# Adding a weight unit from DRAM onto its negated high part: a two-layer encoder on one core

## The chip, the core and the metric

The kernel runs on one core of one Trainium2 chip, as a single program. The metric is the device time of one execution in microseconds (us); lower is better. Five engines work side by side in it: PE multiplies matrices, DVE (vector), ACT (scalar) and POOL (GpSimd) work on tiles, and SP issues transfers from DRAM. Each engine takes its instructions in a fixed order and waits at an instruction until what it needs is there.

## What is computed

The reference is a two-layer encoder over 512 tokens of 1024 features, all in float32. Layer 0 mixes by trailing means and a causal convolution of width 31, layer 1 by chunked attention with 16 heads. Each layer ends in a gated feed-forward part with 2816 hidden features and a sigmoid gate on an input embedding.

```python
for i in range(DEPTH):
    j = i // 2
    if i % 2 == 0:
        mix = pool_conv_mixer(x, mix_w_in[j], pool_w[j], pool_scale[j], conv_dw_w[j],
                              conv_dw_b[j], conv_ln_g[j], conv_ln_b[j], mix_w_out[j])
    else:
        mix = chunked_rel_attention(x, attn_w_qkv[j], attn_rel_bias[j], attn_w_o[j])
    x = layer_norm(DEEPNORM_ALPHA * x + mix, ln_mix_g[i], ln_mix_b[i])
    ffn = conv_ffn(x, ffn_w_up[i], ffn_dw_w[i], ffn_dw_b[i], ffn_w_down[i])
    gate = jax.nn.sigmoid(x @ ple_w_gate[i] + ple_b_gate[i])
    ple = gate * (p[i] @ ple_w_proj[i])
    x = layer_norm(DEEPNORM_ALPHA * x + ffn + ple, ln_ffn_g[i], ln_ffn_b[i])
```

## The kernel before

**Products in three parts.** A float32 value is kept as a high part and a low part, both in the shorter format float32r, whose sum is the value. A product of two such values takes three matmuls (`mm3`, L84 to L86): high by high, low by high, high by low.

**Weights in units.** The weights, 205 units of mostly 128 x 1024 float32 (512 KB), come in the order of their use (the list `order`). The class `Weights` does this for each unit: SP loads it into one of three tiles `wraw` (L138), ACT copies it to `whi`, which rounds it to the high part (L80), and DVE subtracts `whi` from `wraw` and writes the low part `wlo` (L81). The two lines are in the helper `split_into`, which also splits activations, so L80 and L81 stand for those too; the tile names tell them apart. Up to seven units (`NB`) stand split or whole on chip. When the last product on a unit is issued, `free` calls `pump`, which writes the split of the next unit at that place. Units 8 to 11 (`WHOLE`) are loaded without a split.

**The stages.** In layer 0, products for the mixer run while the convolution's 31 taps are worked off in the background: by DVE (L518), and by a product on ACT (L511) with a sum on POOL (L512, 52 sums). DVE adds the two partial results at the end of a channel tile (L523). Then PE takes means over channels by products with ones (L660), DVE subtracts them (L663), and POOL takes the reciprocal root `rs4` (L677). In the feed-forward part every unit serves 24 products.

**The gate pipelines.** Between a mixer or feed-forward part and the stage behind it, `pipeline` works by token tiles of 128: residual sum, LayerNorm (DVE L335 and L336, with a small power on POOL, L330), transposes on PE (L347), and the first products of the next stage. In this stretch the subtract of four units is given to POOL (`W.eng = pool`), so that DVE is free for the LayerNorm.

**Attention.** Layer 1 loops over 16 heads. In one round PE computes scores of head i and transposes the probabilities of head i-1 (L817, tile `s`); ACT copies these to `ph` (L80), copies keys `kk` and queries `qh`, and takes the exponentials (L799); DVE takes a reciprocal `rc` (L801), by which POOL multiplies the four blocks of `s` (L805); PE's transposes of the next round need these. In between PE works through the projection of keys and queries, one unit per round. The order of PE, ACT, DVE and POOL in this part is fixed as written, by `pin`. Elsewhere a scheduler decides the order within each engine when the program is built.

Of the kernel before, what the change touches and what calls it, by code (L numbers as in the profile page):

```python
# [9 lines left out]
F32 = mybir.dt.float32  # L10
# [18 lines left out]
# k-tiles of the hidden layer that are on chip at a time  # L29
CHUNKS = (6, 8, 8)  # L30
# units of weights on chip: split, and as they come from DRAM
NB = 7
NRAW = 3
# the convolution's taps between two output tiles: by the vector engine, and by the scalar and pool engines
TICK = (6, 4)
# units that the splits are written behind while the convolution needs the vector engine
LAG = 2
# products on zeros before the first loads are there
WARM = 2
# units of weights that are used whole, in float32 products, for the vector engine's sake  # L40
WHOLE = (8, 9, 10, 11)
# an order of issue without a wait
# [5 lines left out]
# columns of the per-partition parameters  # L48
# [12 lines left out]
def trunk(ctx, tc, x, xt, pt, cols, w_in, w_pool, w_mo, w_qk, w_v, w_o, relb, rows, w_up, w_dn, w_pp, w_pg, out):  # L61
# [16 lines left out]
    # A float32 value is the exact sum of two float32r parts of 12 bits each.  # L78
# [11 lines left out]
    def pin(engines):  # L90
        """Keeps the order in which the engines' instructions since the last call are written here."""
        ins = nc.cur_bb.bb.instructions
        for eng in engines:
            prev = None
            for i in ins[mark[0] :]:
                if i.engine == eng.engine:
                    if prev is not None:
                        tc.add_manual_dep(i, prev.name, NOSYNC, reason="written order")
                    prev = i
        mark[0] = len(ins)  # L100

# [19 lines left out]
    class Weights:  # L121
        """Units of weights; each is loaded and split NB units ahead of its use."""
# [6 lines left out]
        def piece(self, n, cuts):  # L129
            """Loads unit n, or its part between the last two of the cuts."""  # L130
# [13 lines left out]
        def split(self, cuts=None):  # L144
            """Splits the next unit; with cuts a generator over its pieces."""
# [10 lines left out]
            for c1 in cuts or (n,):  # L156
                split_into(hi[:, c0:c1], lo[:, c0:c1], raw[:, c0:c1], self.eng)
# [31 lines left out]
    def fm_gen(o, a):  # L189
        """One output tile of 128 features with features on partitions; yields halfway."""  # L190
# [17 lines left out]
    def tm_mm(o, t, unit, kk, a, k0, first, last):  # L208
        """o[token, feature] += over k-tile kk of a unit, tokens on partitions."""
# [8 lines left out]
    def tm_units(o, a, ks, nk):  # L218
        """All token tiles, unit by unit, for k-tiles ks of nk; yields after each k-tile."""
# [10 lines left out]
    def tm_first(o, a, nk):  # L230
        """As tm_units for the first unit, a half of the tokens at a time."""
# [13 lines left out]
    class ByToken:  # L245
        """One token tile at a time, over the units of all k-tiles."""
# [19 lines left out]
    def pipeline(acc, pre, tr, mm, ev):  # L266
        """From the last products of a stage over its LayerNorm to the first products of the next, by token tiles."""
# [46 lines left out]
    class Norm:  # L314
        """LayerNorm of r over the features, in place."""
# [43 lines left out]
    class Gate:  # L359
        """r <- alpha r + sigmoid(x @ w_gate + b) * (p @ w_proj), half of the features."""  # L360
# [27 lines left out]
    def mix_to_gate(norm, by, gates):  # L388
        """The mixer's second half of features, LayerNorm and the gate's first half."""
# [13 lines left out]
    def feed_forward(i, nxt):  # L403
        """r <- LN(r + ffn(x)); then the products of nxt, or out."""
# [61 lines left out]
    with tc.tile_pool(name="mix", bufs=1, reuse_waits="tile") as mp:  # L466
        xr = [mp.tile([P, D], F32, tag="pp", name="xr", bufs=4) for _ in range(4)]
        # in the order of their first use
# [14 lines left out]
        # the scalar engine's table and the tensor engine's clock get ready while the first loads run  # L483
# [13 lines left out]
        # vector work that fills the gaps between the splits of the weights  # L497
        bg, convs, hs = deque(), deque(), []

        def tap(on_pool):  # L500
            """One more tap of the first channel tile that has one left: on the vector engine in PSUM, or
            with a product of the scalar engine and a sum of the pool engine."""
# [32 lines left out]
        def conv(c, pv, pg):  # L535
            """Gated linear unit of a channel tile; queues its convolution."""
# [10 lines left out]
        def window(g, pa):  # L547
            """Trailing mean of a channel group minus the group; queued."""
# [29 lines left out]
        # the first two tiles follow x as it comes in  # L578
# [44 lines left out]
        # the layer's input embedding, projected while the convolution runs  # L623
# [31 lines left out]
        # LayerNorm over the convolution's channels, which lie on partitions  # L655
# [13 lines left out]
        # the deviation's reciprocal with tokens on partitions, then again along them  # L669
# [29 lines left out]
    # per pair of heads: A's high part, A's low, B's low, B's high  # L699
# [16 lines left out]
    with tc.tile_pool(name="attn", bufs=1, reuse_waits="tile") as mp:  # L716
# [5 lines left out]
        # per head of a pair: the queries' high part twice; their low part where the keys' high part is, and zeros  # L722
# [5 lines left out]
        # probabilities by keys, the last key block after zeros  # L728
# [12 lines left out]
        def project():  # L741
            """Keys and queries of all pairs; yields after each half of a tile and after its split."""
            for p in range(NP):
# [3 lines left out]
                # a head's high part, and the low part on the other half of the partitions  # L747
# [59 lines left out]
        # keys on partitions, queries from the key's block on  # L807
# [41 lines left out]
        def fill():  # L849
            """Half a tile of projections, or a k-tile of the output projection once these are done."""  # L850
# [44 lines left out]
def _fm(w, np):  # L895
    """[1024, 128 G] -> units of eight k-tiles by 128 columns."""
# [73 lines left out]
```

## Time and profile before

| | before |
|---|---|
| median of 3 runs (lowest to highest), us | 1257.71 (1257.33 to 1257.73) |
| profiled execution: span from first to last instruction, us | 1259.6 |
| PE busy | 1222.5 us, 97% |
| DVE busy | 726.3 us, 58% |
| ACT busy | 490.7 us, 39% |
| POOL busy | 180.3 us, 14% |
| read from DRAM | 122.09 MB |
| share of the transfer engines, load queue | 29.7% |

The profiled execution is one execution apart from the three timed ones, and all durations come from it; the profile gives its span and no further time for it. A busy share is an average over stages with different limits, so PE's 97% leaves some 37 us in which PE is idle, and slower stretches in which the clock granted to it is below 1.00. Of that clock the profile gives the mean in a stretch, as a share of full speed.

### The profile page before, as it was taken

Reading aid. Unit: us, or ns where it says so; the run is one execution under the profiler, and the core shown is the slowest. Engines: PE = TensorE matmul, PEld = TensorE weight load, DVE = VectorE, ACT = ScalarE, POOL = GpSimd, SP = SyncE. Lnnn points to the kernel's source line nnn. Section 1 sums busy time; section 2 is a strip of 40 time slices with the busy share of each in tenths; the row PEclk is TensorE's granted clock in tenths of the full one; section 3 lists DMA queues with packets and bytes.
Section 4 is the critical chain, followed back from the end, with each engine's and each line's share of the span. In section 5 each row is a group of like instructions: output and inputs, shape, how many; then the busy total and the mean of one; then the engine's idle time right before and its main releaser. Section 6 shows DMA issues by size and latency. Waiting matters only on the chain.

```text
span 1259.6 us, 14166 instructions
## 1 busy us (share of the span) xinstructions
PE 1222.5 (97%) x5434; PEld 993.8 (79%) x5434; DVE 726.3 (58%) x1054; ACT 490.7 (39%) x742; POOL 180.3 (14%) x176
## 2 busy tenths in 40 slices
PE   8978999999999999999989999989999999999997
PEld 6735778888888888888878888868888888888886
DVE  6998595544444344449367777595544344434427
ACT  5654433432333123323257777322432233223320
POOL 2994040000000000004012323040000000000001
PEclk9998899999999999999999999999999999999999
DMA  8421232432233222332332232222422332223301
GB/s 308 171 70 50 67 108 77 151 100 88 97 100 101 97 89 99 101 108 97 127 103 76 76 91 78 67 89 96 130 89 99 100 100 92 93 101 100 98 19 67
DMA packets 36643, 125.11 MB, mean 99 GB/s; under 512 B 4064, under 2 KB 4448, under 8 KB 36576
## 3 DMA queue, kind: packets, MB, share of 16 engines
q1 hardware_dynamic: 36576, 124.20, 29.7%
q8 instruction: 43, 0.70, 0.2%
q14 instruction: 24, 0.20, 0.0%
HBM read 122.09 MB, written 2.10 MB: 99 GB/s over the span
## 4 chain that ended last, share of the span: by engine, by line
PE 85%; POOL 5%; DVE 4%; ACT 2%; issue 2%; DMA 1%; SPq 0%; DVEq 0%; POOLq 0%; ACTq 0%
PE psa L84 22%; PE psa L85 22%; PE psa L86 22%; PE psb L86 5%; PE psb L84 5%; PE psb L85 5%; POOL h L512 4%; PE psb L817 2%; DVE r L336 1%; PE psb L786 1%; PE psb L835 1%; PE psb L834 1%; DVE r L335 1%; PE psb L785 1%; POOL s L805 1%
## 5 line engine op out<-in xcount | busy, mean ns | idle before, releaser
L81 DVE TENSOR_TENSOR wlo<-wraw,whi 128x1024 fp32r<-128x1024 f32 (+3 forms) x191 | 239.1, 1252 | 323.5 <-ACT whi L80 317.1
L80 ACT CAST whi<-wraw 128x1024 fp32r<-128x1024 f32 (+2 forms) x203 | 211.6, 1043 | 464.9 <-PE psa L85 235.5
L84 PE MATMUL psa<-a0h,whi 128*128 128x512 f32 x896 | 350.2, 392 | 1.6 <-ACT a0h L80 1.6
L86 PE MATMUL psa<-a0h,wlo 128*128 128x512 f32 x896 | 349.2, 390 | 0.8 <-DVE wlo L81 0.8
L85 PE MATMUL psa<-a0l,whi 128*128 128x512 f32 x896 | 349.2, 390 | 0.0
L84 PEld LDWEIGHTS psa<-a0h,whi 128*128 128x128 f32 x896 | 168.6, 188 | 37.2 <-ACT a0h L80 2.5
L86 PEld LDWEIGHTS psa<-a0h,wlo 128*128 128x128 f32 x896 | 168.4, 188 | 36.6 <-DVE wlo L81 1.2
L85 PEld LDWEIGHTS psa<-a0l,whi 128*128 128x128 f32 x896 | 168.6, 188 | 34.5 <-DVE a0l L81 0.4
L330 POOL TENSOR_TENSOR rs<-ve,nhalf 128x1 f32<-128x1 f32 x16 | 15.1, 941 | 501.7 <-DVE ve L328 501.7
L512 POOL TENSOR_TENSOR h<-h,pr 128x512 f32<-128x512 f32 x52 | 82.7, 1598 | 24.4 <-ACT pr L511 21.3
L422 DVE TENSOR_TENSOR hr<-t,psa 128x512 f32<-128x512 f32 x44 | 30.3, 689 | 86.1 <-PE psa L86 83.1
L84 PE MATMUL psa<-whi,a1h 128*128 128x512 f32 x176 | 71.8, 408 | 6.3 <-ACT a1h L80 5.6
L85 PE MATMUL psa<-wlo,a1h 128*128 128x512 f32 x176 | 70.1, 398 | 0.0
L805 POOL TENSOR_TENSOR s<-s,rc 128x512 f32<-128x512 f32 (+1 forms) x64 | 47.8, 779 | 154.2 <-DVE rc L801 117.0
L86 PE MATMUL psa<-whi,a1l 128*128 128x512 f32 x160 | 63.3, 399 | 2.2 <-DVE a1l L81 2.2
L84 PE MATMUL psb<-whi,a1h 128*128 128x512 f32 x160 | 63.8, 399 | 1.5 <-ACT a1h L651 1.5
L84 PE MATMUL psa<-whi,a0h 128*128 128x512 f32 x160 | 63.7, 398 | 0.0
L85 PE MATMUL psb<-wlo,a1h 128*128 128x512 f32 x160 | 63.2, 395 | 0.0
L85 PE MATMUL psa<-wlo,a0h 128*128 128x512 f32 x160 | 62.9, 393 | 0.0
L86 PE MATMUL psa<-whi,a0l 128*128 128x512 f32 x160 | 62.6, 391 | 0.0
L419 ACT ACTIVATE t<-t 128x512 f32<-128x512 f32 x44 | 27.8, 633 | 89.1 <-DVE t L418 89.1
L86 PE MATMUL psb<-whi,a1l 128*128 128x512 f32 x144 | 56.7, 406 | 1.8 <-DVE a1l L652 1.8
(185 smaller groups left out, 1723.5 us busy)
## 6 DMA issues: line engine op xcount, KB each, us to landing
wraw<-in_w_up SPq DMA_DIRECT2D x88, 512.0 KB, 3.5
wraw<-in_w_dn SPq DMA_DIRECT2D x44, 512.0 KB, 3.5
wraw<-in_w_pg SPq DMA_DIRECT2D x16, 512.0 KB, 3.5
wraw<-in_w_qk SPq DMA_DIRECT2D x16, 512.0 KB, 3.7
wraw<-in_w_mo SPq DMA_DIRECT2D x8, 512.0 KB, 3.5
wraw<-in_w_v SPq DMA_DIRECT2D x8, 512.0 KB, 3.4
bt<-in_relb SPq DMA_DIRECT2D x16, 256.0 KB, 2.6
wraw<-in_w_o SPq DMA_DIRECT2D x8, 512.0 KB, 3.5
```

The costliest lines, as they stand in the source:

```text
L80: act.copy(hi, src)
L81: eng.tensor_tensor(lo, src, hi.bitcast(F32), op=ALU.subtract)
L84: pe.matmul(o, lhsT=ah, rhs=bh, start=first, stop=False)
L85: pe.matmul(o, lhsT=ah, rhs=bl, start=False, stop=False)
L86: pe.matmul(o, lhsT=al, rhs=bh, start=False, stop=last)
L330: pool.tensor_tensor(rs, ve, nhalf, op=ALU.pow)
L335: vec.scalar_tensor_tensor(r[t][:, c], r[t][:, c], mv[:, 0:1], self.g[:, c], op0=ALU.subtract, op1=ALU.mult)
L419: act.activation(t, t, AF.Gelu_apprx_tanh)
L422: vec.tensor_tensor(hr, t, pv, op=ALU.mult)
L512: pool.tensor_tensor(h, h, pr, op=ALU.add)
L805: pool.tensor_tensor(s[:, c], s[:, c], rc[:, b : b + 1].broadcast_to([P, n]), op=ALU.mult)
L817: pe.transpose(bank[:, n : n + P], s[:, SO[b] + j * P : SO[b] + (j + 1) * P], ident)
```

## The change

For the units from number 12 on (`BY_DMA`), the low part is no longer a subtract. ACT copies the raw unit to `whi` as before, then writes `wlo` as `whi` times -1. Then POOL's queue issues a transfer which reads the unit from DRAM once more and adds it onto `wlo`, element by element. What stands there afterwards is the unit minus its high part. The load of the raw unit by SP remains, since the high part is made from it. Units 0 to 7 are split as before.

```diff
+BY_DMA = 12
...
             for c1 in cuts or (n,):
-                split_into(hi[:, c0:c1], lo[:, c0:c1], raw[:, c0:c1], self.eng)
+                if len(self.parts) > BY_DMA:
+                    act.copy(hi[:, c0:c1], raw[:, c0:c1])
+                    act.activation(lo[:, c0:c1], hi[:, c0:c1].bitcast(F32), AF.Copy, scale=-1.0)
+                    nc.gpsimd.dma_start(lo[:, c0:c1], order[len(self.parts) - 1], accum_op=ALU.add)
+                else:
+                    split_into(hi[:, c0:c1], lo[:, c0:c1], raw[:, c0:c1], self.eng)
                 c0 = c1
```

The rest of the diff takes comments out. In the changed file most lines stand seven further down: L512 is L519, L677 is L684, L799 is L806, L330 is L337; the parts of the split are L160 (copy), L161 (negation) and L162 (transfer), and L80 of the activations is L82.

The change moves instructions on every engine. Two places show it. The first is POOL while the convolution runs. Before, its order there has the convolution's sums and little else:

```order
L512 TENSOR_TENSOR h<-h,pr 128x512 x35
L551 MEMSET pa 128x16
L512 TENSOR_TENSOR h<-h,pr 128x512 x9
L551 MEMSET pa 128x16
L512 TENSOR_TENSOR h<-h,pr 128x512 x8
L677 TENSOR_TENSOR rs_988<-ve_986,nhalf 128x4
L330 TENSOR_TENSOR rs<-ve,nhalf 128x1 x2
```

In the changed program POOL issues the transfers in the same order. The first seventeen sums stand ahead of the first of them; this is the end of the stretch, where `in_w_mo` and `in_w_pg` are weights in DRAM:

```order
L519 TENSOR_TENSOR h<-h,pr 128x512 x4
L558 MEMSET pa 128x16
L162 DMA wlo<-in_w_mo 128x1024
L519 TENSOR_TENSOR h<-h,pr 128x512 x5
L162 DMA wlo<-in_w_mo 128x1024
L519 TENSOR_TENSOR h<-h,pr 128x512 x6
L162 DMA wlo<-in_w_mo 128x1024
L519 TENSOR_TENSOR h<-h,pr 128x512 x4
L162 DMA wlo<-in_w_mo 128x1024 x3
L162 DMA wlo<-in_w_pg 128x1024
L684 TENSOR_TENSOR rs_997<-ve_995,nhalf 128x4
L162 DMA wlo<-in_w_pg 128x1024 x2
```

Eight transfers now stand between the sums, and four more between the last sum and the reciprocal root (L677 before, L684 now). On PE, 16 products now stand between the third and the fourth product with ones (L660 before, L667 now), where two stood before.

The second place is a round of attention on ACT. Before, the freed unit's copy comes ahead of the probabilities' copies:

```order
L764 ACTIVATE qh_4302<-psa 64x512
L836 COPY oo<-psb 64x512
L80 CAST whi<-wraw 128x1024
L80 CAST ph<-psb 128x512
L80 CAST ph<-psb 128x384 x2
L750 CAST kk<-psa 64x512 x2
L799 ACTIVATE s,sums<-s,nm 128x512
L799 ACTIVATE s,sums<-s,nm 128x384
L799 ACTIVATE s,sums<-s,nm 128x256
L799 ACTIVATE s,sums<-s,nm 128x128
```

In the changed program the negation stands between them, and the rest of the round is as it was:

```order
L771 ACTIVATE qh_4402<-psa 64x512
L843 COPY oo<-psb 64x512
L160 CAST whi<-wraw 128x1024
L161 ACTIVATE wlo<-whi 128x1024
L82 CAST ph<-psb 128x512
L82 CAST ph<-psb 128x384 x2
L757 CAST kk<-psa 64x512 x2
L806 ACTIVATE s,sums<-s,nm 128x512
L806 ACTIVATE s,sums<-s,nm 128x384
L806 ACTIVATE s,sums<-s,nm 128x256
L806 ACTIVATE s,sums<-s,nm 128x128
```

## Rows read from the trace of the kernel before

**Rows 1.** Page, part 1: busy us, share of the span, instructions.
```profile
PE 1222.5 (97%) x5434; PEld 993.8 (79%) x5434; DVE 726.3 (58%) x1054; ACT 490.7 (39%) x742; POOL 180.3 (14%) x176
```

**Rows 2.** Windows: PE, PEld, DVE, ACT, POOL busy, clock, DMA share, GB/s.
```profile
8.00:12.00 4.00, 2.45 (x10) 1.46 (x8) 2.59 (x4) 2.86 (x5) 0.00 (x0) 1.00 1.01 407
80.00:120.00 40.00, 26.09 (x78) 17.38 (x78) 39.97 (x57) 21.98 (x35) 27.84 (x18) 0.80 0.25 79
180.00:188.00 8.00, 5.81 (x23) 4.68 (x22) 7.97 (x12) 2.97 (x4) 2.71 (x2) 0.79 0.55 181
280.00:320.00 40.00, 40.00 (x178) 33.12 (x177) 15.22 (x18) 9.28 (x10) 0.00 (x0) 1.00 0.29 95
680.00:720.00 40.00, 40.00 (x216) 33.88 (x216) 31.21 (x75) 31.10 (x74) 12.26 (x20) 1.00 0.29 94
```

**Rows 3.** Groups by form: busy us, mean ns | idle us, releaser.
```profile
L81 DVE TENSOR_TENSOR wlo<-wraw,whi 128x1024 fp32r<-128x1024 f32 x186 | 234.6, 1262 | 320.1 <-ACT whi L80 313.7 <-PE psb L817 0.5 <-ACT ph L80 0.3
...
L80 ACT CAST whi<-wraw 128x1024 fp32r<-128x1024 f32 x198 | 208.6, 1053 | 462.4 <-PE psa L85 235.5 <-PE psb L86 114.6 <-PE psa L86 81.0
...
L81 POOL TENSOR_TENSOR wlo<-wraw,whi 128x1024 fp32r<-128x1024 f32 x12 | 31.2, 2618 | 5.1 <-ACT whi L80 5.1
L330 POOL TENSOR_TENSOR rs<-ve,nhalf 128x1 f32<-128x1 f32 x16 | 15.1, 941 | 501.7 <-DVE ve L328 501.7
```

**Rows 4.** One line's instructions, L138: ns min/median/max, first and last start.
```profile
L138 SPq DMA_DIRECT2D wraw<-in_w_up x88: 327/328/473, 179.1 to 1156.0; - x88
```

**Rows 5.** Page, part 6: a load's KB and us to landing.
```profile
wraw<-in_w_up SPq DMA_DIRECT2D x88, 512.0 KB, 3.5
```

**Rows 6.** Timeline of DVE and POOL, convolution: start us, us, ... [idle, releaser].
```profile
95.00 13.97 POOL L512 TENSOR_TENSOR h<-h,pr 128x512 f32<-128x512 f32 x8
...
121.33 0.69 DVE L523 TENSOR_TENSOR h<-h,psb 128x512 f32<-128x512 f32 x1
```

**Rows 7.** One line's instructions, L512.
```profile
L512 POOL TENSOR_TENSOR h<-h,pr x52: 1262/1587/2367, 23.0 to 107.4; 128x512 f32<-128x512 f32 x52
```

**Rows 8.** Timeline, gate pipeline of layer 0: DVE, POOL, PE.
```profile
178.58 3.76 DVE L336 SCALAR_TENSOR_TENSOR r<-r,rs,b 128x512 f32<-128x512 f32 x2
...
176.63 5.16 POOL L81 TENSOR_TENSOR wlo<-wraw,whi 128x1024 fp32r<-128x1024 f32 x2
...
182.49 1.09 PE L347 MATMUL psa<-ident,r 128*128 128x128 f32 x4 [2.19 <-DVE mv L326]
```

**Rows 9.** Timeline, gate pipeline of layer 1: DVE, PE.
```profile
837.15 2.88 DVE L335 SCALAR_TENSOR_TENSOR r<-r,mv,g 128x512 f32<-128x512 f32 x1
...
840.07 0.75 DVE L336 SCALAR_TENSOR_TENSOR r<-r,rs,b 128x512 f32<-128x512 f32 x1
...
841.47 0.66 PE L347 MATMUL psa<-ident,r 128*128 128x128 f32 x4 [1.80 <-DVE a0l L81]
...
850.45 0.66 PE L347 MATMUL psa<-ident,r 128*128 128x128 f32 x4 [0.79 <-DVE a0l L81]
```

**Rows 10.** Timeline, attention: the first head, then one round.
```profile
658.42 0.77 PE L817 MATMUL psb<-ident,s 128*128 128x128 f32 x5 [3.07 <-POOL s L805]
...
704.88 1.05 ACT L80 CAST whi<-wraw 128x1024 fp32r<-128x1024 f32 x1 [1.93 <-PE psa L85]
...
705.02 1.31 PE L817 MATMUL psb<-ident,s 128*128 128x128 f32 x10
...
711.03 3.21 POOL L805 TENSOR_TENSOR s<-s,rc 128x512 f32<-128x512 f32 x4 [5.98 <-DVE rc L801]
...
714.29 1.31 PE L817 MATMUL psb<-ident,s 128*128 128x128 f32 x10
```

**Rows 11.** Timeline, layer 1's second gate: ACT, PE.
```profile
859.59 1.05 ACT L80 CAST whi<-wraw 128x1024 fp32r<-128x1024 f32 x1 [1.38 <-PE psa L86]
...
867.79 0.39 PE L85 MATMUL psa<-wlo,a0h 128*128 128x512 f32 x1
...
870.51 0.39 PE L85 MATMUL psb<-wlo,ph 128*128 128x512 f32 x1
```

## The prediction

> **What bounds the kernel now.** The busy lines first: PE works 97% of the span, DVE 58%, ACT 39%, POOL 14% [rows 1]. So time taken off DVE counts only where PE waits, and the windows say where. In a stretch of the feed-forward part PE is busy 40.00 of 40 us and in attention likewise, while at 80 to 120 us it is busy 26.09 of 40 at a granted clock of 0.80, with DVE at 39.97 [rows 2]. The subtracts that leave DVE are 186 whole units of 1262 ns, 234.6 us in all [rows 3], but the greater part of them lies under a PE that never waits. What remains is to find each place where PE waits for DVE, POOL or ACT, and to price the new chain there.
>
> **What goes, what comes.** For units 12 to 204 (193 of 205) the subtract goes: 181 on DVE and the 12 on POOL, which take 2618 ns each [rows 3]. In their place come 193 negations on ACT, 193 issues on POOL's queue and 193 further reads of a unit from DRAM. Three prices are not in this trace.
> - *Negation*: ACT's copy of the same 128x1024 tile takes 1053 ns [rows 3], and the negation is the same pass with a factor. Bounds 0.95 to 1.2, taken 1.0, since issued one behind the other the two overlap a little.
> - *Issue on POOL*: SP's issue takes 0.33 us [rows 4], POOL's small power 0.94, its own whole-unit subtract 2.62 [rows 3]. An issue works on addresses and not on the elements, so I take 1.0, near POOL's small power.
> - *The summing transfer*: while loads run back to back, the engines move 407 GB/s at share 1.01 [rows 2]. In the feed-forward a unit is 24 products, 24/178 of 40 us = 5.39 us, and the share is 0.29 there: a plain load occupies all engines for 0.29 x 5.39 = 1.56 us. The sum has to read the destination too, so its service lies between 1.56 us (the second read costs nothing) and over twice that. I take 3.1. With a plain load that makes 4.7 of 5.39 us: the feed-forward remains bound by PE. The point at which this fails is 5.39 - 1.56 = 3.83 us.
>
> In the feed-forward, otherwise, nothing is gained or lost: the split units stand six deep ahead, 6 x 5.39 = 32 us, and the new chain of copy, negation, issue and landing takes 1.05 + 1.0 + 1.0 + 3.5 to 5.0 = 6.6 to 8.1 us (3.5 is the landing of a plain load [rows 5]; 5.0 adds 1.5 for the longer service). Without that cover each unit would show its whole chain.
>
> **The convolution (24 to 139 us), -4.** DVE's last tap sum ends at 122.02, POOL's taps at 108.97 [rows 6]; PE's last product with ones (L660) has to wait for that sum. About nine subtracts of DVE between 46 and 115 us, some 14 us, leave. POOL's taps, 1587 ns in the middle against a shortest of 1262 [rows 7], may gain 0.3 each, but eight issues come between them: 8 x 1.0 against some 5 to 6 us gained, so POOL ends at about 111 to 112 and takes the place of DVE; the last sum is ready near 113.7 instead of 122.0. At most 8 to 9 us are to be had. I take half, since in the new order 16 products stand between the third and the fourth product with ones (two before), and four issues stand on POOL ahead of the small power rs (L677), each of which waits for its negation and so for a free unit. Bounds -9 to 0.
>
> **Gate pipeline of layer 0, -3.** POOL subtracts four units there, and beside them DVE's two halves take 3.76 us, 1.88 each, where one alone takes 0.75 [rows 8, 9]; PE waits 2.19 us at 182.49 [rows 8]. In 180 to 188 its clock is 0.79 [rows 2], which is another 0.21 x 8 = 1.7 us. Bounds -3.9 to 0; the subtracts go altogether, so I take most of it.
>
> **Gate pipeline of layer 1, -2.** The same picture: one half on DVE takes 2.88 us beside POOL's subtracts, and PE waits 1.80 and 0.79 us [rows 9]. Bounds -2.6 to 0.
>
> **Attention, +8.5.** One round of the loop, from PE's transposes at 705.02 to the next ones at 714.29, takes 9.3 us, and fourteen such follow the first head. ACT copies the freed unit at 704.88, then the parts of ph, kk and the exponentials; DVE's reciprocal releases POOL's four products at 711.03, which end at 714.24; the transposes start at 714.29 [rows 10]. PE is there 0.05 us after POOL, in nearly every round. So this chain is as long as PE's own work, and PE at 100% busy hides that it has no slack. The order is pinned here, and the negation stands between the copy and ph: ph, the exponentials, POOL's products and the transposes come 1.0 later. The next round's copy is released by PE ahead of those transposes, so its own 1.0 falls on a PE that is already 1.0 late: two rounds share one delay. Seven pairs x 1.0 = 7, and 1.5 for the first head, whose transposes wait 3.07 us for POOL already [rows 10]. Bounds 1 (DVE, freed of its subtract, gives back the time) to 15 (each round pays). The issue on POOL falls into its idle time, about 6 us a round.
>
> **Supply at the gates, +4.** Where four or five units are used side by side, token tile by token tile, they come free together and are needed soon. In layer 1 a copy starts at 859.59 and that unit's low part is used at 867.79, that of the second one after it at 870.51 [rows 11]. New chain: 859.59 + 1.05 + 1.0 + 1.0 + 3.5 to 5.0 = 866.1 to 867.6, just in time; but ACT needs 2.05 us for each further unit and the engines 3.1 + 1.56, against needs (870.51 - 867.79) / 2 = 1.36 us apart, so the third is late by 2 to 3 us. Layer 0 has such a place in its gates and one at V, each smaller. Bounds 0 to 12, taken 4 for all.
>
> **Sum.** -4 - 3 - 2 + 8.5 + 4 = +3.5. On the profiled span of 1259.6 us this gives 1263.1; that span is 1.9 us above the median of the runs (1257.71), so the time forecast is 1261. The five bounds added up would be -14 to +27; as they are independent I take 1253 to 1272 for this case.
>
> **Where a page speaks against the change.** The row on transfers gives only a lower bound for the sum [rows 2]. The Trainium skill, "Collectives: The Full Stack", section "The bandwidth ceiling: the fold count and why AG ≠ RS ≠ AR", says of reductions done by the transfer engines that the addition costs no time by itself but needs two source reads, and so runs at half the rate of a copy. No run here shows it; by it the service would be 3.1 us, an estimate, and the sum as above.
>
> **Rivals.**
> - *The transfers become the bound* (slower). If the addition takes three times a plain load, 4.68 us, then a unit needs 4.68 + 1.56 = 6.24 us of the engines against 5.39 of PE. The 132 feed-forward units lose 0.85 each: +112, about 1370. For it: nothing here sums in a transfer, and 3.83 us is only a quarter above my value. Against it: two reads alone do not reach it. 0.15.
> - *Attention pays almost nothing* (the other side). If DVE, which loses 1.26 us a round, brings the reciprocal and the bank copies as much earlier as the negation delays them, the +8.5 falls to +2: -4 - 3 - 2 + 2 + 4 = -3, about 1254.5. It decides when less than 0.3 us of the 1.0 comes through per pair. For it: DVE is busy 31.21 of 40 us there [rows 2]. Against it: from ph to the exponentials the chain is all ACT, and its next wait, 5.98 us, is POOL's [rows 10]. 0.16.
> - *The issue is long* (slower). If an issue holds POOL 2.6 us, as its own subtract does, then 8 x 2.6 stand between the convolution's taps: POOL ends near 124, the convolution gives +2 instead of -4, the gates keep their waits (+5), and supply costs 3 more: about 1275. For it: POOL's subtracts and DVE's work stretch each other [rows 8, 9]. Against it: an issue reads no tile. 0.07.
>
> The Trainium skill, "SBUF — State Buffer", section "SBUF: two separate sides", supports the last one: descriptors of a transfer issued by GpSimd can't be written while DVE runs in a mode that holds both ports. No row here has such an issue; if it held for DVE's work at 80 to 120 us, the time would be that of this rival.
>
> **Chances.** The forecast 0.62, rivals 0.15, 0.16, 0.07. A measurement of this kernel tells about 0.2%, 2.5 us, from no change. Of the forecast's 0.62, 0.08 is faster, 0.18 the same, 0.36 slower (1253 to 1272 around 1261); the transfers and the issue are slower, attention's rival is faster. Faster 0.24, same 0.18, slower 0.58. The range runs from 1251, which takes in attention's rival, to 1300, which takes in the long issue and a small excess of the transfers; what lies outside is nearly all of the first rival.
>
> **What the profile after would show.** DVE near 490 us busy, ACT near 685, the read volume near 223 MB. In the feed-forward window PE busy 40 of 40 with a DMA share near 0.87: a share of 1.0 there, with PE waiting for wlo, is the first rival. In attention a period of 9.7 to 9.9 us with ACT's negation ahead of ph; 9.3 is the second. In the convolution POOL's last tap ends at 111 to 112 (past 120 is the third), and DVE's last sum ends before 115. At the gates PE waits for wlo released by a transfer. I would be wrong above all by the price of the addition, which no row shows.

## The result, and the profile after

The changed kernel takes 1277.01 us (median of 4 runs, 1275.45 to 1281.89) against 1257.52 for the kernel before: 1.0147 times, 95% interval 1.0114 to 1.018, or 19.5 us more. The page of the profiled execution (span 1275.7 us) begins as follows; its first line answers to [rows 1].

```profile
PE 1220.8 (96%) x5434; PEld 992.0 (78%) x5434; DVE 502.1 (39%) x873; ACT 678.7 (53%) x935; POOL 309.7 (24%) x357
...
HBM read 223.02 MB, written 2.10 MB: 176 GB/s over the span
...
wlo<-in_w_up POOLq DMA_DIRECT2D x88, 512.0 KB, 5.8
...
wlo<-in_w_pg POOLq DMA_DIRECT2D x16, 512.0 KB, 8.7
```

DVE lost 224 us of work, ACT gained 188, and PE, which bounds the kernel, has the same 5434 products as before. The span grew by 16.1 us, and PE's idle time from 37.1 to 54.9 us, so the loss is in waits of PE. Two of the three prices that no row of before showed can now be read: the groups by form have the negation (L161) and the issue (L162).

```profile
L161 ACT ACTIVATE wlo<-whi 128x1024 fp32r<-128x1024 f32 x192 | 202.5, 1056 | 2.6
...
L162 POOL DMA_DIRECT2D wlo<-in_w_up x88 | 76.6, 870 | 392.2 <-ACT wlo L161 328.0 <-PE psa L87 34.9 <-issue 22.3
```

The negation takes 1.06 us and the issue 0.87, where 1.0 was taken for each. The third price follows from the windows that answer to [rows 2].

```profile
80.00:120.00 40.00, 24.92 (x77) 16.04 (x76) 35.16 (x48) 27.03 (x42) 28.80 (x22) 0.87 0.46 114
180.00:188.00 8.00, 6.66 (x31) 5.55 (x32) 4.42 (x7) 2.89 (x4) 0.89 (x1) 1.00 1.05 273
280.00:320.00 40.00, 40.00 (x178) 33.14 (x177) 6.26 (x10) 17.02 (x18) 6.96 (x8) 1.00 0.83 197
680.00:720.00 40.00, 37.77 (x204) 31.91 (x203) 24.45 (x67) 33.12 (x71) 16.53 (x26) 1.00 0.53 132
```

In the feed-forward (280 to 320) PE is still busy 40.00 of 40 us, with the transfer share at 0.83 instead of 0.29: the sum occupies the engines for (0.83 - 0.29) x 5.39 = 2.9 us a unit, under the 3.83 at which it would have become the bound. In attention (680 to 720), where PE was busy 40.00 of 40, it is now busy 37.77. That is the first place of loss. Comparing the times of the same instructions in the two traces gives the balance by stage:

| point in the program | before | after | later by | of this in the stage |
|---|---|---|---|---|
| reciprocal root of the convolution's norm (L677, now L684) | 134.5 | 135.2 | 0.7 | +0.7 |
| first feed-forward activation (L416, now L423) | 229.9 | 231.6 | 1.7 | +1.0 |
| first scores of attention (L785, now L792) | 643.8 | 646.0 | 2.2 | +0.5 |
| last transposes of attention (L817, now L824) | 797.9 | 808.8 | 10.9 | +8.7 |
| last transposes of layer 1's gate pipeline (L347, now L354) | 850.8 | 859.2 | 8.4 | -2.5 |
| last feed-forward activation | 1203.5 | 1219.9 | 16.4 | +8.0 |
| end of the span | 1259.6 | 1275.7 | 16.1 | -0.3 |

Attention first. The timeline of one round, engine by engine, answers to [rows 10]:

```profile
691.22 1.05 ACT L160 CAST whi<-wraw 128x1024 fp32r<-128x1024 f32 x1 [2.05 <-PE psa L87]
692.30 1.06 ACT L161 ACTIVATE wlo<-whi 128x1024 fp32r<-128x1024 f32 x1
693.38 1.35 ACT L82 CAST ph<-psb 128x512 fp32r<-128x512 f32 x3
...
698.41 3.23 POOL L812 TENSOR_TENSOR s<-s,rc 128x512 f32<-128x512 f32 x4 [3.75 <-DVE rc L808]
...
701.70 0.55 PE L824 MATMUL psb<-ident,s 128*128 128x128 f32 x3 [1.12 <-POOL s L812]
...
710.92 1.26 PE L824 MATMUL psb<-ident,s 128*128 128x128 f32 x10
```

The negation stands between the copy and ph, and PE's transposes at 701.70 wait 1.12 us for POOL's products. At 710.92, one round later, they don't wait, and so it goes on: waits of 1.07 to 1.12 us at 682.00, 701.70, 721.38, 741.09, 760.77 and 780.48, one in every second round, 6.6 us in all.

The rest of the +8.7 is mostly at the first head, and there it is the granted clock. Its transposes wait for POOL as long as before (3.13 us, 3.07 in [rows 10]), but the ten of them take 2.38 us where they took 1.31, and the clock is 0.83 in 660 to 670 (1.00 in the same stretch before). From these transposes to the next ones PE takes 10.87 us instead of 9.25, 1.6 more. Three of the runs below (late units, descriptors, convolution) leave attention as it is here and have no such stretch at the first head; from the first scores to the last transposes they take 161.1 to 161.2 us, 7.0 more than the 154.1 before. Two runs without a transfer in attention have the stretch (2.40 us for the ten transposes with attention's units by subtract, 2.39 with the feed-forward alone), so it is not the change that brings it. One more wait stands before the loop, for ACT's copy of the first queries, and was not there before:

```profile
646.04 0.49 PE L792 MATMUL psb<-kk,qh 128*128 128x512 f32 x1 [1.11 <-ACT qh L767]
...
660.69 2.38 PE L824 MATMUL psb<-ident,s 128*128 128x128 f32 x10 [3.13 <-POOL s L812]
```

The second place is the gates. PE waits there for low parts that a transfer has yet to bring, eight times: 1.57 and 1.19 us in layer 0, 0.62 at V, and in layer 1 1.76 and 2.15 in the first gate and 3.05, 0.99 and 2.11 in the second, 13.4 us in all. The timeline of the second gate of layer 1 answers to [rows 11]:

```profile
867.70 1.05 ACT L160 CAST whi<-wraw 128x1024 fp32r<-128x1024 f32 x1 [1.38 <-PE psa L88]
...
870.25 0.91 POOL L162 DMA_DIRECT2D wlo<-in_w_pg  x1 [22.79 <-PE psa L87]
872.28 0.87 POOL L162 DMA_DIRECT2D wlo<-in_w_pg  x1 [1.12 <-ACT wlo L161]
874.31 0.86 POOL L162 DMA_DIRECT2D wlo<-in_w_pp  x1 [1.15 <-ACT wlo L161]
879.38 0.86 POOL L162 DMA_DIRECT2D wlo<-in_w_up  x1 [4.21 <-issue]
...
879.12 0.75 PE L87 MATMUL psa<-wlo,a0h 128*128 128x512 f32 x1 [3.05 <-DMA wlo<-in_w_pg]
...
883.00 0.50 PE L87 MATMUL psa<-wlo,a0h 128*128 128x512 f32 x1 [0.99 <-DMA wlo<-in_w_pg]
...
886.76 0.50 PE L87 MATMUL psb<-wlo,ph 128*128 128x512 f32 x1 [2.11 <-DMA wlo<-in_w_pp]
```

The first unit's transfer is issued at 870.25, 2.55 us after its copy began, as the chain of copy, negation and issue has it. But it lands only at 879.1, 8.9 us later, and the next two 3.8 to 3.9 us apart, while PE needs them 1.36 us apart. In 867 to 890 us PE is busy 16.84 of 23 us at a granted clock of 0.93, where before it was busy throughout at 1.00: 6.2 us of waits and 0.07 x 23 = 1.6 us of clock make up nearly all of the +8.0 of that stage.

The gains are there as well. None of the waits of [rows 8] and [rows 9] for the LayerNorm is left in this trace: no wait of PE for DVE above 0.3 us in either gate pipeline. The kernel before had two more in layer 1, which [rows 9] do not show, so that 2.19 + 0.92 + 0.79 + 1.80 + 0.79 = 6.5 us are gone:

```profile
822.29 0.66 PE L347 MATMUL psa<-ident,r 128*128 128x128 f32 x4 [0.92 <-DVE r L336]
823.74 1.04 PE L347 MATMUL psa<-ident,r 128*128 128x128 f32 x4 [0.79 <-DVE r L336]
```

The clock is back as well: it was 0.83 in 180 to 190 and in 820 to 830 before and is 1.00 in both now, 1.7 us each.

The growth of the spans, 16.1 us, is less than that of the medians, 19.5. In the runs of the changed kernel the time is the span plus 1.8 us (1277.46 for the profiled 1275.7), so the profiled execution of the kernel before took about 1261.4, which is 3.9 above its median. Where these 3.9 us lie in that one execution can't be told.

### The profile page after: what moved, and what is told of

Same layout as the page of the kernel before. It is cut to its first block, busy times and chain, and to the rows that moved or that the text cites. A ratio compares the mean times of both kernels' runs of the same rounds, so it can differ in the third digit from the quotient of the medians.

```text
span 1275.7 us, 14493 instructions
## 1 busy us (share of the span) xinstructions
PE 1220.8 (96%) x5434; PEld 992.0 (78%) x5434; DVE 502.1 (39%) x873; ACT 678.7 (53%) x935; POOL 309.7 (24%) x357
## 4 chain that ended last, share of the span: by engine, by line
PE 75%; issue 6%; DMA 4%; POOL 2%; ACT 2%; DVE 0%; DVEq 0%; POOLq 0%
PE psa L87 19%; PE psa L86 19%; PE psa L88 19%; PE psb L87 5%; PE psb L86 5%; PE psb L88 5%; DMA wlo<-in_w_pp 2%; POOL s L812 2%; DMA wlo<-in_w_pg 1%; PE psb L824 1%; ACT wlo L161 1%; ACT whi L160 1%; POOL wlo L162 1%; DMA wlo<-in_w_v 1%; PE psb L842 1%
## 5 line engine op out<-in xcount | busy, mean ns | idle before, releaser
L160 ACT CAST whi<-wraw 128x1024 fp32r<-128x1024 f32 x193 | 202.0, 1049 | 359.1 <-PE psa L87 190.0
L161 ACT ACTIVATE wlo<-whi 128x1024 fp32r<-128x1024 f32 x193 | 203.2, 1054 | 2.6
L162 POOL DMA_DIRECT2D wlo<-in_w_up x88 | 76.6, 870 | 392.2 <-ACT wlo L161 328.0
L424 DVE SCALAR_TENSOR_TENSOR t<-psa,cst,t 128x511 f32<-128x511 f32 x44 | 33.0, 749 | 207.9 <-ACT t L423 207.9
L162 POOL DMA_DIRECT2D wlo<-in_w_dn x44 | 38.3, 869 | 199.9 <-ACT wlo L161 199.9
L519 POOL TENSOR_TENSOR h<-h,pr 128x512 f32<-128x512 f32 x52 | 78.3, 1526 | 30.1 <-ACT pr L518 27.7
```

The costliest lines, as they stand in the source:

```text
L160: act.copy(hi[:, c0:c1], raw[:, c0:c1])
L161: act.activation(lo[:, c0:c1], hi[:, c0:c1].bitcast(F32), AF.Copy, scale=-1.0)
L162: nc.gpsimd.dma_start(lo[:, c0:c1], order[len(self.parts) - 1], accum_op=ALU.add)
L424: vec.scalar_tensor_tensor(t[:, 1:], pg[:, : S - 1], col(wc + 1), t[:, 1:], op0=ALU.mult, op1=ALU.add)
L519: pool.tensor_tensor(h, h, pr, op=ALU.add)
```

## The experiments

The theory (A) after the result: attention pays because ACT's negation lengthens the chain that PE's transposes wait for, the gates pay because low parts land late, and the convolution and the feed-forward neither pay nor gain. The rivals: the doubled transfers cost wherever they run (B); POOL's small room for transfer descriptors holds them up (C). Every ratio below is to the kernel before, run on the same chip; the runs of the kernel before had medians of 1257.5 to 1260.5 us there. The edits are against the changed kernel. Where a set of units is given, the test in the split becomes the one by number that the first edit shows; it is not shown again.

**Attention's units by subtract.** In the changed kernel, the set of units made by transfer is

```diff
-BY_DMA = 12
+BY_DMA = set(range(12, 205)) - set(range(105, 129))
...
-                if len(self.parts) > BY_DMA:
+                if len(self.parts) - 1 in BY_DMA:
```

> The changed kernel, but units 105 to 128 (keys, queries and the output projection, whose splits stand in the attention loop) are split by copy and DVE subtract as before. Theory A (the negation on ACT lengthens the chain that attention waits for): the six waits of 1.10 us before the transposes go, the round returns to 9.3 us a head, and the time falls by 8 us, to about 1269. Rival B (the loss comes from the doubled transfers, wherever they are late): attention keeps most of its waits, since the loads around it stay; the time falls by less than 3 us.

Measured: 1268.3 us, 1.0057 (1.0038 to 1.0076). From 1.0147 this is 11 us less where 8 were expected (the spans of the profiled executions differ by 10.0), and the six waits are gone, with the one at the first queries; PE is busy 40.00 of 40 us again at 680 to 720. From the first scores to the last transposes it is 156.6 us, 6.2 less than in the changed kernel; a further 3.1 us of the spans' difference lie before the first scores, the wait for the queries among them. So the loss in attention hangs on those units; whether on the negation or on the transfer, the next run tells.

**Attention's negation on DVE.** All transfers stay.

```diff
-                    act.activation(lo[:, c0:c1], hi[:, c0:c1].bitcast(F32), AF.Copy, scale=-1.0)
+                    if len(self.parts) - 1 in range(105, 129):
+                        vec.tensor_scalar(lo[:, c0:c1], hi[:, c0:c1].bitcast(F32), -1.0, None, op0=ALU.mult)
+                    else:
+                        act.activation(lo[:, c0:c1], hi[:, c0:c1].bitcast(F32), AF.Copy, scale=-1.0)
```

> The changed kernel, but for units 105 to 128 the negation runs on DVE in place of ACT; the summing transfers all stay. Theory A (ACT's negation is what attention pays): as in the run with subtracts there, 1269, a round of 9.3 us. Rival B (the transfer's latency or traffic in attention): 1277 as the changed kernel, since every transfer remains and the low parts come no earlier.

Measured: 1268.69 us, 1.0062 (1.0044 to 1.0079), the same as with subtracts. Its window (columns as in [rows 2]):

```profile
680.00:720.00 40.00, 40.00 (x216) 33.96 (x215) 28.19 (x73) 31.24 (x75) 15.96 (x25) 1.00 0.63 152
```

And from its timeline one round on ACT, and the transposes of the next:

```profile
686.19 1.05 ACT L160 CAST whi<-wraw 128x1024 fp32r<-128x1024 f32 x1 [2.00 <-PE psa L87]
687.26 1.35 ACT L82 CAST ph<-psb 128x512 fp32r<-128x512 f32 x3
...
695.59 1.31 PE L827 MATMUL psb<-ident,s 128*128 128x128 f32 x10
```

The transfer share is 0.63 (0.53 in the changed kernel), so the transfers are all there; ph follows the copy at once, and the transposes don't wait. From the first scores to the last transposes it is 154.2 us, against 154.1 in the kernel before. What attention paid for is the 1.06 us on ACT; rival B falls there.

**The late units by subtract.** The eight units whose low part PE waited for, on POOL or DVE as before:

```diff
-BY_DMA = 12
+BY_DMA = set(range(12, 205)) - {26, 30, 100, 132, 133, 136, 137, 138}
```

> The changed kernel, but the eight units whose low part PE waited for (26, 30, 100, 132, 133, 136, 137, 138) are split by copy and subtract, on POOL or DVE as before. Theory A (at the gates units come free together and the transfers land late): the eight waits, 13.4 us in all, go; some 3 us of them come back as waits for DVE beside POOL's subtracts, so the time falls by about 10 us, to 1267. Rival B (the stretch is bound by DVE's LayerNorm and the waits only change their name): less than 4 us is won.

Measured: 1262.13 us, 1.001 (0.9996 to 1.0024). That is 17 us less than the changed kernel, more than the 10 expected. (Its span, 1257.7, is 18 less, but that execution was 2.7 us faster than the median of its twelve, and 1.6 us of the difference are the first head's clock.) All eight waits are gone, with the stretch of lower clock at the second gate, and the waits for DVE, of which I had expected 3 us back, did not return. At the second gate PE is busy throughout:

```profile
858.00:880.00 22.00, 22.00 (x98) 18.21 (x97) 9.82 (x13) 9.16 (x10) 1.77 (x2) 1.00 0.64 168
```

The next unit at V, 101, is now late by 1.25 us, a new wait. So eight units of 193 carry most of the loss, and the rival, that the waits only change their name, falls.

**Transfers by themselves.** A kernel of its own moves units of the same size; the encoder is left out.

```python
for i in range(6):
    pool.dma_start(L[i], w[9 + i], accum_op=ALU.add)
sync()
...
for i in range(6):
    nc.sync.dma_start(F[i], w[21 + i])
    pool.dma_start(L[i], w[27 + i], accum_op=ALU.add)
sync()
```

> Not the encoder: transfers of one 512 KB unit alone, its output is left out (zeros and sums in its place). One plain load and six in a row, one summing transfer and six in a row, six copies by POOL's queue without a sum, six sums beside six plain loads, six sums while DVE subtracts tile from tile. Theory A (a sum costs the engines twice a plain load, and POOL can have only a few in flight): six sums in a row end 2.6 to 3.1 us apart against 1.3 for loads, the fourth issue waits for the first landing; beside loads the sums end about 4 us apart. Rival B (POOL's issue is the limit): the sums end as far apart as the copies by POOL's queue. With DVE busy the issues stay at 0.9 us by A; a rule that DVE blocks them would make them 1.5 us and more.

A small DVE operation waits for each landing, so its start tells when a unit is there. First two plain loads out of six, then the first four of six sums, and POOL's issues of these; then sums beside loads, with the issue of the first three; last, the issues of six copies by POOL's queue without a sum and the first landing of these:

```profile
43.20 0.16 DVE L82 TENSOR_TENSOR gate<-gate,f 128x1 f32<-128x1 f32 x1 [1.64 <-DMA f<-in_w_up]
44.48 0.16 DVE L82 TENSOR_TENSOR gate<-gate,f 128x1 f32<-128x1 f32 x1 [1.12 <-DMA f<-in_w_up]
...
66.50 0.16 DVE L80 TENSOR_TENSOR gate<-gate,lo 128x1 f32<-128x1 f32 x1 [5.57 <-DMA lo<-in_w_up]
68.95 0.16 DVE L80 TENSOR_TENSOR gate<-gate,lo 128x1 f32<-128x1 f32 x1 [2.30 <-DMA lo<-in_w_up]
71.44 0.16 DVE L80 TENSOR_TENSOR gate<-gate,lo 128x1 f32<-128x1 f32 x1 [2.33 <-DMA lo<-in_w_up]
75.43 0.16 DVE L80 TENSOR_TENSOR gate<-gate,lo 128x1 f32<-128x1 f32 x1 [3.83 <-DMA lo<-in_w_up]
...
60.94 2.68 POOL L99 DMA_DIRECT2D lo<-in_w_up  x3 [7.88 <-DVE lo L86]
66.66 0.88 POOL L99 DMA_DIRECT2D lo<-in_w_up  x1 [3.04 <-DVE gate L80]
...
96.06 2.70 POOL L108 DMA_DIRECT2D lo<-in_w_up  x3 [9.98 <-DVE lo L86]
105.91 0.16 DVE L80 TENSOR_TENSOR gate<-gate,lo 128x1 f32<-128x1 f32 x1 [9.96 <-DMA lo<-in_w_up]
109.73 0.16 DVE L80 TENSOR_TENSOR gate<-gate,lo 128x1 f32<-128x1 f32 x1 [3.66 <-DMA lo<-in_w_up]
...
82.63 3.45 POOL L103 DMA_DIRECT2D lo<-in_w_up  x6 [10.17 <-DVE lo L86]
86.26 0.16 DVE L80 TENSOR_TENSOR gate<-gate,lo 128x1 f32<-128x1 f32 x1 [3.68 <-DMA lo<-in_w_up]
```

Loads follow each other at 1.28 us (one gap of the five is 2.5), sums at 2.5 (the fourth, issued late, comes 4.0 behind the third), sums beside loads at 3.82, which is the two added (1.28 + 2.5 = 3.78); this holds for the first gaps, and as the loads run out the last three are 3.5, 2.3 and 2.8. The last four copies by POOL's queue without a sum came 1.25 to 1.28 us apart, so it is the addition that costs, and not POOL. Three sums are issued at once, and the fourth, at 66.66, right behind the first landing; of the copies without a sum all six are issued, by 86.08, before the first has landed.

A sum alone takes 5.7 us from the start of its issue (52.05) to its landing (57.78), the first of six 5.6 (60.94 to 66.50): the sums behind it don't delay it. Beside loads it takes from 96.06 to 105.91, 9.9 us. The gate shows nearly the same: 8.9 us for the first, 3.8 for each further one. There SP issues five loads of the feed-forward's units between 868.8 and 880 us, in the midst of the sums. So the loads are the likely cause of the late first landing; no run of the encoder held them back to show it. The last part, with DVE at work, told nothing, since DVE's subtracts ran long before the transfers.

**More room for descriptors.**

```diff
-dynamic_dma_scratch_size=1024
+dynamic_dma_scratch_size=2048
```

> The changed kernel with twice the room for POOL's transfer descriptors (1024 to 2048 bytes), so that about six summing transfers instead of three can be under way. Theory A (at the gates the engines' rate is the limit, 2.5 us a sum and 1.3 us a load): the fourth issue comes earlier, but the low parts land no earlier; the time stays within 3 us of the changed kernel, 1.012 to 1.017 times the kernel before. Rival C (the small ring holds the transfers up): the waits at the gates fall by half and the time by 6 us, to 1.010 or less.

Measured: 1275.79 us, 1.0127 (1.0105 to 1.0148). POOL's waits without a visible cause fall from 33.8 to 0.6 us, so the room was what held the fourth issue. But at the second gate of layer 1 PE waits 1.96, 1.86 and 0.85 us and still 1.41 and 2.15 at the first, the eight places together 10.7 instead of 13.4 us, and the time is that of the changed kernel within the intervals. C falls as the cause of the loss.

**The convolution's units by subtract.**

```diff
-BY_DMA = 12
+BY_DMA = set(range(12, 205)) - set(range(12, 26))
```

> The changed kernel, but units 12 to 25, which are split while the convolution runs, by copy and subtract. Theory A (the convolution won 2.6 us of DVE's time at its last tap sum and gave it back behind POOL's issues, 0.7 us later at the reciprocal root): nearly the same time as the changed kernel, 1.013 to 1.016 times the kernel before. The prediction's term (4 us won there): 1.018.

Measured: 1275.51 us, 1.012 (1.0098 to 1.0142), as the run above on the same chip. The convolution gains nothing from the transfers, and the value of 1.018 that the prediction's term asks for is excluded. That DVE's 2.6 us were given back behind POOL's issues, as expected here, the trace does not bear out; the rows stand with the prediction's terms below.

**The feed-forward alone.**

```diff
-BY_DMA = 12
+BY_DMA = set(range(31, 97)) | set(range(139, 205))
```

> Only the 132 feed-forward units (31 to 96 and 139 to 204) by negation and summing transfer, all others by subtract. Theory A (the feed-forward hides the whole chain, 2.5 + 1.3 us of transfer under 5.39 us of PE): 1.000 times the kernel before, at most 2 us off, with PE busy 40.00 of 40 us. Rival B (the doubled traffic costs something with each unit): two thirds of the loss, 1.008 to 1.010.

Measured: 1260.93 us, 1.0003 (0.9986 to 1.002). 132 units, two thirds of the change, cost nothing and bring nothing, at a transfer share of 0.87 and PE at 40.00 of 40 us in the same window. With this B falls altogether.

```profile
280.00:320.00 40.00, 40.00 (x178) 33.15 (x177) 6.26 (x10) 17.23 (x18) 6.98 (x8) 1.00 0.87 198
```

**Both causes undone.** Attention's 24 units and the late ones, with unit 101, by subtract; 160 remain by transfer.

```diff
-BY_DMA = 12
+BY_DMA = set(range(12, 205)) - set(range(105, 129)) - {26, 30, 100, 101, 132, 133, 136, 137, 138}
```

> Attention's units 105 to 128 and the nine late ones (26, 30, 100, 101, 132, 133, 136, 137, 138) by subtract, the rest by negation and summing transfer. Theory A (the two causes add up and nothing else is lost): 8 and 17 us less than the changed kernel, and 1 more for unit 101: 0.993 to 0.996 times the kernel before, since DVE's and POOL's waits at the gates stay away. Rival: the gate stretches were only shifted and show up elsewhere, 0.999 to 1.002.

Measured: 1252.83 us, 0.995 (0.9934 to 0.9966), faster than both kernels. Between 140 and 960 us only the first head's 3.07 us and one of 0.81 at the end of attention are left of PE's waits above 0.5 us. From the single runs 1.0147 - 0.009 - 0.0137 = 0.992 would follow; each of these ratios is known to 0.001 to 0.003 only, and within that the two causes add up.

**Seven of POOL's twelve units, alone,** and all other units as in the kernel before: first by transfer, then on DVE without one.

```diff
-BY_DMA = 12
+BY_DMA = {27, 28, 29, 102, 103, 134, 135}
```

> The kernel before, with only seven of POOL's twelve units (27, 28, 29, 102, 103, 134, 135, split in the gate pipelines and at V) by negation and summing transfer. Theory A (all that the change wins lies there, where POOL's subtracts slowed DVE's LayerNorm and PE waited 2.19, 0.92, 0.79, 1.80 and 0.79 us): 0.993 to 0.996 times the kernel before, as the run that keeps the convolution and the feed-forward by transfer too. Rival (a good part of that run's gain comes from the convolution): 0.997 to 0.999.

Measured: 1256.22 us, 0.9961 (0.9942 to 0.9979).

```diff
-BY_DMA = 12
+BY_DMA = 205
...
-                split_into(hi[:, c0:c1], lo[:, c0:c1], raw[:, c0:c1], self.eng)
+                split_into(hi[:, c0:c1], lo[:, c0:c1], raw[:, c0:c1], vec if len(self.parts) - 1 in (27, 28, 29, 102, 103, 134, 135) else self.eng)
```

> The kernel before, with the same seven units subtracted on DVE in place of POOL, and no summing transfer at all. Theory A (the transfer is what helps, since it leaves DVE free in the LayerNorm): seven subtracts of 1.26 us stand in DVE's way there, and the time is that of the kernel before, 0.999 to 1.002. Rival (only POOL's use of the tiles hurts, and DVE has the time): as with the transfer, 0.993 to 0.996.

Measured: 1259.11 us, 0.9983 (0.9966 to 1.0). The seven units bring the greater part of the gain by themselves, 5 us by the ratio (3.4 by the medians). Without a transfer, on DVE, the value lies between: the two intervals overlap, so how much comes from POOL leaving the tiles alone and how much from DVE's free time stays open in the times. The traces say a little more: layer 0's wait of 2.19 us is gone in both runs, so there it is enough that POOL leaves the tiles alone; of the last two waits in layer 1 (1.80 and 0.79 us in the kernel before) the run on DVE still has 0.97 and 0.82, the run by transfer none. Both keep 0.9 and 0.8 us earlier in layer 1 and have a third wait of 2.6 us there that the profile of the kernel before does not show. The run with both causes undone has none of these; which of its further units takes them away wasn't separated.

**Does DVE hold up POOL's issue?** A second kernel of its own, three sums at a time: while DVE is idle, while it subtracts tile from tile, while it copies tile to tile.

```python
for i in range(3):
    pool.dma_start(L[i], w[21 + i], accum_op=ALU.add)
for i in range(24):
    vec.tensor_copy(G[i % 2], gate)
```

> Not the encoder: its output is left out, zeros and sums in its place. Three summing transfers with DVE idle, three while DVE subtracts tile from tile, three while DVE copies tile to tile. If DVE blocks POOL's issue (the rule behind the prediction's third rival), the issues beside DVE's work take 1.5 us and more, most of all beside the copies; if not, 0.9 to 1.0 us as in the changed kernel.

```profile
16.36 2.80 POOL L94 DMA_DIRECT2D lo<-in_w_up  x3 [15.92 <-DVE lo L88]
29.80 2.68 POOL L98 DMA_DIRECT2D lo<-in_w_up  x3 [10.63 <-DVE lo L88]
46.60 16.32 POOL L104 DMA_DIRECT2D lo<-in_w_up  x3 [14.12 <-DVE lo L88]
...
46.46 14.53 DVE L106 COPY g<-gate 128x1024 f32<-128x1024 f32 x24
```

The rows are POOL's three issues with DVE idle, beside subtracts and beside copies, and DVE's copies. Beside subtracts three issues take 2.68 us as with DVE idle (2.80); beside copies 16.32, and of these the first issue alone takes 14.52, until DVE's 24 copies are through. So DVE does hold up POOL's issue, but with copies, and no issue of the changed kernel met such a stretch: the longest of the 193 took 1.02 us.

## Why the prediction was right, and where its sizes were off

The direction and the range held: slower, 1277 within 1251 to 1300. The value, 1261, was 16 us short, and 1277 lies beyond the 1253 to 1272 given for the likeliest case. It lies in the part of the range that was added for a long issue and for an excess of the transfers, and neither occurred; that the rival of the long issue was priced at 1275 is a coincidence, since an issue took 0.87 us. So the range held in part by luck. The mechanisms were the ones named; two terms had the wrong size and one the wrong sign. Against the spans, on which the sum was made:

| term | forecast | measured |
|---|---|---|
| convolution | -4 | +0.7 |
| gate pipelines of layers 0 and 1 | -3 - 2 | -6.7 (16.1 - 0.7 - 8.7 - 13.4, by difference) |
| attention | +8.5 | +8.7 |
| supply at the gates | +4 | +13.4 |
| sum | +3.5 | +16.1 |

- *Attention.* Right in its mechanism and its pattern: one delay for two rounds, as the negation on DVE shows it to be ACT's alone. The rival in which DVE gives the time back is out. That the size agrees is partly luck: the seven pairs at 1.0 became six waits, 6.6 us, and the 1.5 for a longer wait at the first head did not come (3.13 against 3.07 us). In this execution 1.6 us of lower clock stood in its place; without it the stage pays 7.0.
- *Supply at the gates.* This is the step that failed. The chain to the start of the issue was right to 0.5 us; issue and landing were taken as 1.0 + 3.5 to 5.0 us, a plain load's time with its own longer service. From the start of the issue to the landing 8.9 were measured, and 11.4 for the whole chain from the copy, where 6.6 to 8.1 were taken. A sum alone would have been inside this (5.7 in the transfer kernel); what was left out is that the first sum already shares the engines with the loads of the next stage, which SP issues at the same moment (9.9 beside loads). I had priced this sharing for the spacing of the units only (3.1 + 1.56, measured 3.8 to 3.9). The bound of 12 was short of the 13.4, and the clock lost after such waits (1.6 us at one gate) was not counted at all.
- *Convolution.* DVE's last tap sum came earlier, but by 2.6 us and not by 8:

```profile
118.77 0.67 DVE L530 TENSOR_TENSOR h<-h,psb 128x512 f32<-128x512 f32 x1
...
113.17 2.65 POOL L519 TENSOR_TENSOR h<-h,pr 128x512 f32<-128x512 f32 x2 [1.95 <-ACT pr L518]
116.31 1.27 POOL L519 TENSOR_TENSOR h<-h,pr 128x512 f32<-128x512 f32 x1 [0.48 <-ACT pr L518]
```

  POOL's last tap ends at 117.6, where the prediction had 111 to 112 and [rows 6] have 108.97. POOL now waits four times for ACT's products, 5.5 us in all, which the step on the convolution left out. That the negations in ACT's queue cause this is not shown: ahead of the product for the longest of these waits, ACT itself stood idle for DVE for 2.80 us.

```profile
111.31 0.62 ACT L82 CAST a1h<-pd 128x512 fp32r<-128x512 f32 x1 [2.80 <-DVE pd L576]
```

  What was won was then lost in PE's order, the reason for which the prediction took half. The first two rows are of the kernel before, the others of the changed one:

```profile
125.83 1.02 PE L660 MATMUL psa<-h,ones 128*128 128x512 f32 x2
130.55 3.63 PE L673 MATMUL psa<-ones,sq 128*128 128x1 f32 x32
...
124.50 1.02 PE L667 MATMUL psa<-h,ones 128*128 128x512 f32 x2
131.30 3.63 PE L680 MATMUL psa<-ones,sq 128*128 128x1 f32 x32
135.21 1.04 POOL L684 TENSOR_TENSOR rs<-ve,nhalf 128x4 f32<-128x4 f32 x1 [0.30 <-DVE ve L682]
```

  The last products with ones start only 1.3 us earlier, behind the 16 others, and those on the squares 0.75 later, since other products of PE take 6.8 us between the two where they took 4.7. The reciprocal root then waits for DVE's `ve`, and not for the four issues on POOL, the last of which is over at 134.9. The +0.7 itself is within what executions differ by: in the runs that split the convolution's units as here, the root starts between 133.9 and 136.2.
- *Gate pipelines.* Right, and more than forecast: of the five waits that are gone (6.5 us) the prediction had read three, and layer 1 won more than its bound of 2.6, 4.3 us of waits and 1.7 of clock. The -6.7 is only what remains of the 16.1, so the clock lost at the gates and the wait for the first queries are in it. The run with seven units by transfer shows that this gain stands alone.
- *The transfers as the bound.* The service of a sum is 2.5 us alone and 2.9 by the feed-forward's share, under the 3.83 of the rival and near the 3.1 taken; the feed-forward run shows it free. The Trainium skill, "Collectives: The Full Stack", section "The bandwidth ceiling: the fold count and why AG ≠ RS ≠ AR", has for reductions in collectives that an addition needs two source reads and so runs at half the rate of a copy; the sums here agree, 2.5 against 1.28 us.
- *The issue.* 0.87 us, the rival with 2.6 is out. The Trainium skill, "SBUF — State Buffer", section "SBUF: two separate sides", says that GpSimd can't write a transfer's descriptors while DVE runs an operation that holds both ports, such as a float32 copy from tile to tile. The second transfer kernel agrees, with 16.32 us for three issues beside copies against 2.80 with DVE idle; beside DVE's subtracts they took 2.68.

## What to carry to other kernels

A resource that is busy half the time may still be the one that everything waits for in a stretch: one more microsecond on ACT in attention's fixed chain cost as much as the whole change could win, and it cost it in pairs of rounds. When work is moved to transfers, price the landing of the first one beside the loads of the next stage, and not a lone transfer; keep a subtract on an engine for units that come free shortly before their use. Apply such a change where its price is hidden and its gain is not: here nine units at the gates and the 24 of attention, of 193, made the difference between 1.0147 and 0.995.

## What was unexpected of the hardware

Summing transfers and plain loads don't overlap: sums follow each other at 2.5 us, loads at 1.28 us and mixed ones at 3.82 us a pair. With 1024 bytes for descriptors three sums of 512 KB were under way, and the next issue came only when the first had landed (issue at 66.66 us, landing at 66.50), while six copies without a sum were issued ahead of the first landing; with 2048 bytes POOL's waits of this kind in the encoder fell from 33.8 to 0.6 us. And a stretch of DVE copies from tile to tile stopped POOL's issue, 14.52 us for the first of three, while beside DVE subtracts with two operands three took 2.68 us together.
